# Strided attention on one core: the first fourteen output groups are stored one by one instead of in pairs

## The chip, the cores and the metric

The kernel runs on one core of a Trainium2 chip. Its time is the device time of one execution in microseconds (us). A core has five engines with a stream of instructions each: PE (TensorE, matrix products), DVE (VectorE), ACT (ScalarE), POOL (GpSimd) and SP (SyncE), which here only issues transfers. The transfers are carried out by sixteen DMA engines; SP's instruction ends when a transfer has been handed over, and a semaphore tells later that its data has landed.

## The reference

Every query of a head attends to 16 keys, the rows 0, 64, 128, ... of that head:

```
batch, heads, seq, dim = (8, 12, 1024, 64); stride = 64; float32
for i in range(seq):
    attend_positions = np.arange(0, seq, stride)
    q = Q[:, :, i:i + 1, :]
    k, v = K[:, :, attend_positions, :], V[:, :, attend_positions, :]
    scores = np.einsum('bhqd,bhkd->bhqk', q, k) / sqrt(dim)
    weights = softmax(scores over the 16 keys)
    result[:, :, i, :] = np.einsum('bhqk,bhkd->bhqd', weights, v)
```

So all of Q (96 heads of 256 KB) has to be read and an output of the same size written, and of K and V only 1/64 of the rows.

## The kernel before

**Groups.** The 96 heads are taken four at a time: 24 groups (NG), each with 1 MB of Q and 1 MB of output. K's and V's rows are fetched once, as 384 KB each in rows of 256 bytes.

**A group's way through the core.** SP loads the group's Q into one of ten buffers `qn` (QBUFS = 10). ACT and POOL cast a half each to bfloat16 (L328, L330), DVE transposes (L335, in the loop L449), PE makes the scores (L469), ACT raises them in two halves (L353), PE multiplies with the values in three blocks (L497), and DVE (L453, L459), ACT (L383) and POOL (L385) scale the blocks into one of eight output buffers `out_sb` (OBUFS = 8). POOL's L385 is a group's last work; a store waits for it. Cast, transposition and scores run up to three groups ahead of the outputs.

**What gives buffers back.** A load into `qn` waits until the casts of the group ten earlier are done. The second half of the exponential of group g (L353) waits until the store of group g - 8 has landed; everything that writes the output buffer comes after it. The map `stored` holds which transfer that is.

**The order on SP.** Every transfer goes through SP, which issues strictly in the order of the program. First come K's rows, load 0, V's rows and loads 1 to 9. Then, for each group g in turn, load g + 10 (while g + 10 < 24), and after every second group one store of two groups, 2 MB (two neighbouring output buffers are one tile, so one access pattern covers both). Groups 22 and 23 are stored alone; the last of them stands outside the planned part, at L512. A transfer that waits holds up every later one on SP, loads too.

**Semaphores.** Each load buffer and each pair of output buffers has a semaphore (`lane`) of its own; K's and V's loads borrow two of the stores'. The waits are worked out from the reads and writes that each operation declares (`Program.plan`).

Of the kernel before, what the change touches and what calls it, by code (L numbers as in the profile page):

```python
# [18 lines left out]
def _ap_with(ap: bass.AP, new_ap, extra_offset: int = 0) -> bass.AP:  # L19
    return dataclasses.replace(  # L20
        ap, ap=[list(p) for p in new_ap], offset=ap.offset + extra_offset
    )


def _copy(nc, out: bass.AP, in_: bass.AP):

    sides = [
        mybir.BassSymbolicTensorAccessPattern(
            ap=side.ap, dtype=side.dtype, bass_ap=side,
            is_dma=True, for_custom_bir_dma=True,  # L30
        )
        for side in (in_, out)
    ]
    return nc.sync.add_instruction(
        mybir.InstDMACopy(
            name=nc.get_next_instruction_name(), engine=mybir.EngineType.SP,
            ins=sides[:1], outs=sides[1:], queue="qSPDynamicHW",
            mode="Copy",
        )
    )  # L40


class Program:
# [13 lines left out]
    def op(self, engine, fn, reads=(), writes=(), after=(), lane=None, gate=None, gates=(), looped=False, last=False):  # L57
        i = len(self.ops)
        deps, own = set(after), set()
        for k in reads:  # L60
            deps.add(self.writer.get(k))
            own.add(self.writer.get(k))
        for k in writes:
            deps.update(self.readers.get(k, ()))
            deps.add(self.writer.get(k))
            own.add(self.writer.get(k))
        deps.discard(None)
        for k in reads:
            self.readers.setdefault(k, []).append(i)
        for k in writes:  # L70
            self.writer[k], self.readers[k] = i, []
        self.ops.append(dict(
            engine=engine, fn=fn, lane=lane or engine, deps=deps, own=own,
            gate=gate, gates=gates, last=last, looped=looped or engine == "PE",
        ))
        return i
# [90 lines left out]
def kernel(  # L167
# [16 lines left out]
    NG = B * H // HG  # L184
# [6 lines left out]
    QBUFS = 10  # L191
    OBUFS = 8
# [5 lines left out]
    k_raw = sb.tile([P, NC, D], FP32, name="k_raw")  # L198
    v_raw = sb.tile([P, NC, D], FP32, name="v_raw")
# [22 lines left out]
    op = prog.op  # L222
# [3 lines left out]
    def load(g):  # L226
        n = P if g < 2 else 32
        op("SP", lambda: _copy(
            nc, qn[g % QBUFS],
            _ap_with(Q, [[HG * SD // n, n], [1, HG * SD // n]], g * HG * SD),  # L230
        ), writes=[f"qn{g % QBUFS}{h}" for h in range(2)], lane=f"q{g % QBUFS}")
# [3 lines left out]
    def load_rows(name, tile_, src, lane):  # L235
        op("SP", lambda: nc.sync.dma_start(tile_, _ap_with(src, kv_src)),  # L236
           writes=[name], lane=lane)

    load_rows("k_raw", k_raw, K, f"out{OBUFS // 2 - 2}")
    load(0)  # L240
    load_rows("v_raw", v_raw, V, f"out{OBUFS // 2 - 1}")
    for g in range(1, QBUFS):
        load(g)

# [2 lines left out]
        out=identity, in_=identity, compare_op=ALU.not_equal, fill=1.0, base=0,  # L247
# [3 lines left out]
    for c in range(2):  # L251
        for a in range(2):
            op("POOL", lambda c=c, a=a: nc.gpsimd.tensor_copy(
                out=perm_v[:, c, a],
# [8 lines left out]
        out=s_sel, in_=identity.rearrange("p (h s k) -> p s h k", h=2, s=4),  # L263
        op=ALU.max, axis=mybir.AxisListType.XY,
    ), reads=["identity"], writes=["s_sel"])
    op("POOL", lambda: nc.gpsimd.tensor_copy(  # L266
        out=v_all[:, :, 4 * D :], in_=s_sel.unsqueeze(1).to_broadcast([P, 4, 4])
    ), reads=["s_sel"], writes=["ones"])
    op("POOL", lambda: nc.gpsimd.tensor_copy(
        out=mask, in_=s_sel.unsqueeze(2).to_broadcast([P, 4, D])  # L270
# [45 lines left out]
    def values(g):  # L316
        v = v_bufs[g % 4]
        op("POOL", lambda: nc.gpsimd.tensor_tensor(  # L318
            out=v[:, 0 : 4 * D].rearrange("p (s d) -> p s d", s=4), in0=mask,
            in1=v_rep[:, g // 2, g % 2].unsqueeze(1).to_broadcast([P, 4, D]),  # L320
            op=ALU.mult,
        ), reads=["mask", "v_rep0", "v_rep1"], writes=[f"v{g % 4}"], gate="masked")
# [3 lines left out]
    def cast(g):  # L326
        q, b = qn[g % QBUFS], qb[g % 2]
        op("ACT", lambda: nc.scalar.copy(b[:, half:], q[:, half:]),  # L328
           reads=[f"qn{g % QBUFS}1"], writes=[f"qb{g % 2}1"])
        op("POOL", lambda: nc.gpsimd.tensor_copy(out=b[:, 0:half], in_=q[:, 0:half]),  # L330
           reads=[f"qn{g % QBUFS}0"] + [f"qb{g % 2}1"] * (g >= 2) + ["turn"] * (g < 2),
           writes=[f"qb{g % 2}0"] + ["turn"] * (g < 2), gate="cast")
# [4 lines left out]
    def transpose(g):  # L337
        k_in = {0: "00", 1: "01"}.get(g)
        op("DVE", lambda: turn_over(g),
           reads=[f"qb{g % 2}0", f"qb{g % 2}1"] + [f"k_t{k_in}{s}" for s in range(4) if k_in],  # L340
           writes=[f"qt{g % 2}"], gate="turned", gates=[("cast", g + 1)], looped=g >= 2)

    def scores(g):
        s = g % 2
        op("PE", None,
           reads=[f"qt{g % 2}"] + [f"k_t{int(min(g, NG - 1) >= 8)}{g % 2}{i}" for i in range(4)],
           writes=[f"sc{s}0", f"sc{s}1"], gates=[("turned", g + 1)])
        if g == NG:
            return
        sc, w = sc_ps[s], w_bufs[g % 2]  # L350
        for a in range(2):
            wa = w[64 * a : 64 * a + 64]
            op("ACT", lambda a=a, wa=wa: nc.scalar.activation(  # L353
                out=_ap_with(wa, [wa.ap[0], [P, 8], [1, 2], [2, 32]], extra_offset=64 * a),
                in_=sc[64 * a : 64 * a + 64].rearrange("p (t x q) -> p t x q", t=8, x=2),
                func=AF.Exp, bias=0.0, scale=scale,
            ), reads=[f"sc{s}{a}"], writes=[f"w{g % 2}{a}"], gate="raised" if a else None,
               after=[stored[g - OBUFS]] if a and g >= OBUFS else [])
# [8 lines left out]
    def outputs(g, c):  # L367
        t = (3 * g + c) % 2
        o_key, to_key = f"o{(3 * g + c) % 2}", f"out{g % OBUFS}{c}"
        op("PE", None, reads=[f"w{g % 2}0", f"w{g % 2}1", f"v{g % 4}", "ones"], writes=[o_key],  # L370
           gates=[
               [("raised", g + 1), ("masked", g + 2), ("scaled", 2 * g + 2)],
               [("copied", g + 1)], [("scaled", 2 * g + 3)],
           ][c], gate="out")
        r, o, to, by = parts(g, c)
        r_key = f"rec{g % 2}{c}"
        sums = op("DVE", None, reads=[o_key], writes=[r_key], gates=[("out", 3 * g + c + 3)],
                  gate="own" if c < 2 else None, looped=True)
        if c < 2:
            op("DVE", None, reads=[o_key, r_key], writes=[to_key], gate="scaled",  # L380
               gates=[("own", 2 * g + c + 1)], looped=True)
        else:
            op("ACT", lambda: nc.scalar.copy(to, o), reads=[o_key], writes=[to_key, f"copy{g}"],  # L383
               after=[sums])
            op("POOL", lambda: nc.gpsimd.tensor_tensor(out=to, in0=to, in1=by, op=ALU.mult),  # L385
               reads=[to_key, r_key], writes=[to_key], last=g == NG - 1)

    def send(g, n):
        o = out_sb[g % OBUFS]
        return _copy(  # L390
            nc,
            _ap_with(out, [[16 * D, P], [2 * SD, 2 * n], [1, 16 * D]], g * HG * SD),
            _ap_with(o, [o.ap[0], [1, 1], [1, 32 * n * D]]),
        )

    def store(g, n):
        both = range(g, g + n)
        sent = op("SP", lambda: send(g, n), lane=f"out{g % OBUFS // 2}",
                  reads=[f"out{i % OBUFS}{c}" for i in both for c in range(3)])
        stored.update((i, sent) for i in both)  # L400

# [22 lines left out]
    for g in range(NG):  # L424
        transpose(g + 2)
        if g + 3 < NG:
            cast(g + 3)
        elif g + 1 < NG:
            op("POOL", lambda: nc.gpsimd.nop(), reads=[f"out{(g - 1) % OBUFS}2"], gate="cast")
        if g + 2 < NG:  # L430
            values(g + 2)
        scores(g + 1)
        for c in range(3):
            outputs(g, c)
        if g + 1 < NG:
            op("ACT", lambda: nc.scalar.nop(), reads=[f"copy{g}"], gate="copied")
        if g + QBUFS < NG:
            load(g + QBUFS)
        if g % 2 and g < NG - 2:
            store(g - 1, 2)  # L440
        elif g == NG - 2:
            store(g, 1)

    def dve_stream(sems, gates):
        dve = nc.vector
# [101 lines left out]
```

## Time and profile before

| | |
|---|---|
| three runs | 127.96, 128.0 and 128.7 us; median 128.0 |
| the profiled execution | 127.91 us, of which its first to its last instruction (the span) take 126.1 |
| bytes moved | 51.15 MB: 25.95 read from HBM, 25.17 written |
| granted TensorE clock, mean | 0.883 |
| transfers | 24 loads of 1 MB, 11 stores of 2 MB, 2 stores of 1 MB, K's and V's rows |

The page of the profile gives the busy time of each engine and, in forty slices of the span, the share in which the sixteen DMA engines were busy. The median time from a transfer's issue to its landing was 15.8 us for the loads, 16.6 for the stores of 2 MB and 7.5 for the two of 1 MB. That time holds the wait behind earlier transfers as well as the transfer itself, so it is no measure of a transfer's own length; that is read from the distance between one landing and the next.

### The profile page before, as it was taken

To read this page: it belongs to the slowest core of one execution; us is meant where nothing else is said; L and a number is where in the kernel's file an instruction comes from. 1 tells how busy PE (TensorE), PEld (TensorE's weight loads), DVE (VectorE), ACT (ScalarE), POOL (GpSimd) and SP (SyncE) were. 2 spreads that over 40 slices of the span, in tenths; PEclk is the share of its full clock that TensorE was granted. 3 is DMA by queue.
4 is the path that set the end of the run, shared out by engine and by line. 5 is a ranking of instruction groups with operands and counts; after the bars stand their busy time and mean duration, and the time that the engine had idled before them with its cause. 6 is when DMAs were issued, how large, how long until landed. Compare 5 with 4: busy or idle time off the path is not lost.

```text
span 126.1 us, 1274 instructions
## 1 busy us (share of the span) xinstructions
PE 67.0 (53%) x296; PEld 29.4 (23%) x296; DVE 90.8 (72%) x161; ACT 80.9 (64%) x103; POOL 78.1 (62%) x89
## 2 busy tenths in 40 slices
PE   0005463877946656777655666366277659662000
PEld 0001121433413322333322333132032224330000
DVE  2996356786697999696997999989467746996000
ACT  4260944469667999957899799797199097562000
POOL 4073338278569799949699699979269359344300
PEclk9999999999999999756999999999756855999555
DMA  1999999899999999989989989999999999999992
GB/s 38 346 356 514 416 416 468 385 478 416 416 400 442 436 400 462 436 374 468 416 374 442 452 364 431 473 385 426 447 410 421 426 426 426 431 421 426 413 421 125
DMA packets 6324, 51.15 MB, mean 406 GB/s; under 512 B 3696, under 2 KB 3696, under 8 KB 3696
## 3 DMA queue, kind: packets, MB, share of 16 engines
q1 hardware_dynamic: 6320, 51.12, 97.0%
q14 instruction: 4, 0.03, 0.1%
HBM read 25.95 MB, written 25.17 MB: 405 GB/s over the span
## 4 chain that ended last, share of the span: by engine, by line
DMA 26%; DVE 24%; PE 19%; POOL 10%; ACT 8%; issue 4%; SPq 2%; DVEq 0%; ACTq 0%; POOLq 0%
DMA out_dram<-out_sb 19%; DVE out_sb L459 14%; PE sc L469 10%; PE o L497 9%; DMA qn<-in_Q_dram 7%; DVE qt L335 6%; POOL out_sb L385 5%; ACT out_sb L383 4%; DVE rec L453 4%; POOL qb L330 3%; ACT w_all L353 3%; ACT qb L328 2%; SPq L236 1%; DVE v_rep L312 1%; POOL v_all L318 1%
## 5 line engine op out<-in xcount | busy, mean ns | idle before, releaser
L497 PE MATMUL o<-v_all,w_all 128*128 128x260 bf16 x192 | 38.6, 322 | 30.3 <-DVE out_sb L459 25.1
L385 POOL TENSOR_TENSOR out_sb<-out_sb,rec 128x768 f32<-128x768 f32 x24 | 35.3, 1472 | 28.0 <-ACT out_sb L383 28.0
L469 PE MATMUL sc<-qt,k_t 128*128 128x512 bf16 x100 | 34.0, 472 | 16.5 <-DVE qt L335 12.3
L353 ACT ACTIVATE w_all<-sc 64x512 bf16<-64x512 f32 x48 | 35.2, 733 | 11.1 <-DMA out_dram<-out_sb 7.1
L459 DVE TENSOR_TENSOR out_sb<-o,rec 128x768 f32<-128x768 f32 (+1 forms) x48 | 39.6, 824 | 1.6
L335 DVE STREAM_TRANSPOSE qt<-qb 128x1024 int32<-128x1024 int32 x26 | 31.7, 1220 | 3.8 <-POOL qb L330 3.5
L497 PEld LDWEIGHTS o<-v_all,w_all 128*128 128x128 bf16 x192 | 17.9, 110 | 54.8 <-DVE out_sb L459 33.5
L383 ACT COPY out_sb<-o 128x768 f32<-128x768 f32 x24 | 19.2, 799 | 15.3 <-DVE rec L453 15.0
L328 ACT CAST qb<-qn 128x1024 bf16<-128x1024 f32 x24 | 25.0, 1045 | 4.5 <-DVE v_rep L312 1.7
L330 POOL CAST qb<-qn 128x1024 bf16<-128x1024 f32 x24 | 24.8, 1038 | 2.1 <-DMA qn<-in_Q_dram 2.1
L453 DVE RECIPROCAL rec<-o 128x12 f32<-128x12 f32 (+1 forms) x72 | 15.2, 211 | 13.8 <-PE o L497 13.2
L318 POOL TENSOR_TENSOR v_all<-mask,v_rep 128x256 bf16<-128x256 bf16 x24 | 16.1, 671 | 4.2 <-DVE v_rep L312 4.1
L469 PEld LDWEIGHTS sc<-qt,k_t 128*128 (+1 forms) x100 | 11.1, 112 | 28.1 <-issue 12.3
L257 DVE MEMSET k_t<- 128x3600 uint32 x1 | 3.1, 3058 | 2.3 <-issue 2.3
L312 DVE CAST v_rep<-o 128x768 bf16<-128x768 f32 x2 | 1.9, 938 | 2.9 <-PE o L302 2.9
L291 DVE COPY k_t<-k_r 32x256 bf16<-32x256 bf16 x8 | 3.1, 394 | 0.1
L277 ACT CAST k_bf<-k_raw 128x256 bf16<-128x256 f32 (+1 forms) x2 | 0.9, 508 | 2.8 <-DMA k_raw<-in_K_dram 2.8
L266 POOL COPY v_all<-s_sel 128x16 bf16<-128x16 bf16 x1 | 0.2, 197 | 3.7 <-DVE s_sel L262 3.7
L302 PE MATMUL o<-v_bf,perm_v 128*128 128x384 bf16 x4 | 1.5, 521 | 1.3 <-POOL v_bf L416 1.3
L277 ACT ACT_TABLE_LOAD x1 | 1.3, 1283 | 1.3 <-SPq L143 1.3
L291 ACT COPY k_t<-k_r 32x128 bf16<-32x128 bf16 x4 | 1.2, 295 | 0.5 <-DVE k_r L279 0.5
L291 POOL COPY k_t<-k_r 32x128 bf16<-32x128 bf16 x4 | 1.2, 288 | 0.3
(13 smaller groups left out, 5.1 us busy)
## 6 DMA issues: line engine op xcount, KB each, us to landing
qn<-in_Q_dram SPq DMA_DIRECT2D x24, 1024.0 KB, 15.8
out_dram<-out_sb SPq DMA_DIRECT2D x11, 2048.0 KB, 16.6
out_dram<-out_sb SPq DMA_DIRECT2D x2, 1024.0 KB, 7.5
k_raw<-in_K_dram SPq DMA_DIRECT2D x1, 384.0 KB, 4.5
v_raw<-in_V_dram SPq DMA_DIRECT2D x1, 384.0 KB, 7.0
```

The costliest lines, as they stand in the source:

```text
L291: op(e, lambda: fn(k_t[dst : dst + 32, 2 * part.start + c : 2 * part.stop : 2, :, col : col + NK], k_r[src : src + 32, part].rearrange("p ...
L318: op("POOL", lambda: nc.gpsimd.tensor_tensor(out=v[:, 0 : 4 * D].rearrange("p (s d) -> p s d", s=4), in0=mask, in1=v_rep[:, g // 2, g % 2] ...
L328: op("ACT", lambda: nc.scalar.copy(b[:, half:], q[:, half:]), reads=[f"qn{g % QBUFS}1"], writes=[f"qb{g % 2}1"])
L330: op("POOL", lambda: nc.gpsimd.tensor_copy(out=b[:, 0:half], in_=q[:, 0:half]), reads=[f"qn{g % QBUFS}0"] + [f"qb{g % 2}1"] * (g >= 2) + [ ...
L335: return nc.vector.transpose(qt[g % 2].bitcast(I32), qb[g % 2].bitcast(I32))
L353: op("ACT", lambda a=a, wa=wa: nc.scalar.activation(out=_ap_with(wa, [wa.ap[0], [P, 8], [1, 2], [2, 32]], extra_offset=64 * a), in_=sc[64 ...
L383: op("ACT", lambda: nc.scalar.copy(to, o), reads=[o_key], writes=[to_key, f"copy{g}"], after=[sums])
L385: op("POOL", lambda: nc.gpsimd.tensor_tensor(out=to, in0=to, in1=by, op=ALU.mult), reads=[to_key, r_key], writes=[to_key], last=g == NG - 1)
L453: sums = dve.reciprocal(r, o_ps[(3 * j + c) % 2][:, 0 : blocks[c][1], 4 * D : 4 * D + 4])
L459: dve.tensor_tensor(out=to, in0=o, in1=by, op=ALU.mult).then_inc(gates["scaled"], 1)
L469: r = pe.matmul(sc_ps[g % 2], lhsT=k_t[:, k, f, NK * (1 - e) : NK * (1 - e) + P], rhs=_ap_with(qt[g % 2], [qt[g % 2].ap[0], [D, 8], [16 * ...
L497: r = pe.matmul(o_ps[(3 * j + c) % 2][:, i, 0 : 4 * D + 4], lhsT=w_bufs[j % 2][:, i0 + i], rhs=v_bufs[j % 4], start=True, stop=True,)
```

## The change

Groups 0 to 13, the ones behind which a load is still to be issued, are stored singly, right behind that load. SP's order in the middle becomes load 10, store 0, load 11, store 1, ... load 23, store 13, and then as before: pairs 14-15, 16-17, 18-19, 20-21, and 22 and 23 alone. In the order before it was load 10, load 11, store 0-1, load 12, load 13, store 2-3, and so on. There are eight semaphores for the stores, one for each output buffer, instead of four, and K's and V's loads borrow the last two of them. Each of the groups 8 to 21 now waits for the store of one group. The instructions of PE, DVE, ACT and POOL are the same and stand in the same order; only which semaphore some of ACT's wait for differs. SP issues seven transfers more.

```
-    load_rows("k_raw", k_raw, K, f"out{OBUFS // 2 - 2}")
+    load_rows("k_raw", k_raw, K, f"out{OBUFS - 2}")
     load(0)
-    load_rows("v_raw", v_raw, V, f"out{OBUFS // 2 - 1}")
+    load_rows("v_raw", v_raw, V, f"out{OBUFS - 1}")
...
     def store(g, n):
         both = range(g, g + n)
-        sent = op("SP", lambda: send(g, n), lane=f"out{g % OBUFS // 2}",
+        sent = op("SP", lambda: send(g, n), lane=f"out{g % OBUFS}",
                   reads=[f"out{i % OBUFS}{c}" for i in both for c in range(3)])
         stored.update((i, sent) for i in both)
...
         if g + QBUFS < NG:
             load(g + QBUFS)
-        if g % 2 and g < NG - 2:
+        if g < NG - QBUFS or g == NG - 2:
+            store(g, 1)
+        elif g % 2 and g < NG - 2:
             store(g - 1, 2)
-        elif g == NG - 2:
-            store(g, 1)
```

## The prediction

> **What bounds the kernel now.** I read the page first, for the engine nearest to full.
>
> ```profile
> span 126.1 us, 1274 instructions
> PE 67.0 (53%) x296; PEld 29.4 (23%) x296; DVE 90.8 (72%) x161; ACT 80.9 (64%) x103; POOL 78.1 (62%) x89
> DMA  1999999899999999989989989999999999999992
> q1 hardware_dynamic: 6320, 51.12, 97.0%
> ```
>
> No engine is over 72%, but the sixteen DMA engines are busy for 97.0% of the span, idle only in the first and the last slice. SP has one queue, so the question is whether it ever ran dry. The next view is SP's timeline (start, duration, what is issued), and beside it the time to landing of single transfers, each from a look at the one in whose window the issue falls. The rows of the second fence belong to the issues at 11.00 (load 10), 25.92 (load 11), 30.43, 39.26, 46.73, 53.47, 103.96, 111.57, 114.76 and 118.49 us, in this order.
>
> ```profile
> 11.00 0.52 SPq L34 DMA_DIRECT2D qn<-in_Q_dram  x1
> 25.92 0.47 SPq L34 DMA_DIRECT2D qn<-in_Q_dram  x1
> 30.43 0.63 SPq L34 DMA_DIRECT2D out_dram<-out_sb  x1
> 39.26 0.59 SPq L34 DMA_DIRECT2D out_dram<-out_sb  x1
> 46.73 0.59 SPq L34 DMA_DIRECT2D out_dram<-out_sb  x1
> 53.47 0.59 SPq L34 DMA_DIRECT2D out_dram<-out_sb  x1
> 103.96 0.54 SPq L34 DMA_DIRECT2D out_dram<-out_sb  x1
> 111.57 0.54 SPq L34 DMA_DIRECT2D out_dram<-out_sb  x1
> 114.76 0.54 SPq L34 DMA_DIRECT2D out_dram<-out_sb  x1
> 118.49 0.54 SPq L34 DMA_DIRECT2D out_dram<-out_sb  x1
> ```
>
> ```profile
> qn<-in_Q_dram SPq DMA_DIRECT2D x1, 1024.0 KB, 22.6
> qn<-in_Q_dram SPq DMA_DIRECT2D x1, 1024.0 KB, 10.1
> out_dram<-out_sb SPq DMA_DIRECT2D x1, 2048.0 KB, 10.9
> out_dram<-out_sb SPq DMA_DIRECT2D x1, 2048.0 KB, 12.1
> out_dram<-out_sb SPq DMA_DIRECT2D x1, 2048.0 KB, 14.4
> out_dram<-out_sb SPq DMA_DIRECT2D x1, 2048.0 KB, 17.6
> out_dram<-out_sb SPq DMA_DIRECT2D x1, 2048.0 KB, 11.6
> out_dram<-out_sb SPq DMA_DIRECT2D x1, 2048.0 KB, 8.9
> out_dram<-out_sb SPq DMA_DIRECT2D x1, 1024.0 KB, 8.1
> out_dram<-out_sb SPq DMA_DIRECT2D x1, 1024.0 KB, 6.9
> ```
>
> Issue plus landing time gives when each landed: load 10 at 33.6, load 11 at 36.0, store 0-1 at 41.3, then 51.4, 61.1 and 71.1; at the end store 18-19 at 115.6, 20-21 at 120.5, 22 at 122.9 and 23 at 125.4. The first store was issued at 30.43, when the queue still held work until 36.0, 5.6 us; the last at 118.49, when store 22 had yet to land at 122.9, 4.4 us. These are the thinnest places, so the queue never ran dry, and the time is the sum of what each transfer takes of the DMA engines. The chain of waits (start, length, what) gives the two more landings that the prices need, load 1 at 3.22 + 8.47 = 11.7 and store 12-13 at 76.75 + 24.06 = 100.8:
>
> ```profile
> 3.22 8.47 DMA qn<-in_Q_dram
> 76.75 24.06 DMA out_dram<-out_sb
> ```
>
> **Prices.** Nine loads from load 1 to load 10: (33.6 - 11.7) / 9 = 2.43 us for 1 MB with loads alone. Stores of 2 MB alone: (115.6 - 100.8) / 3 = 4.93. Stores of 1 MB alone: (125.4 - 120.5) / 2 = 2.45. In the mixed stage a round of two loads and a 2 MB store, landing to landing, takes (100.8 - 41.3) / 6 = 9.92, against 2 x 2.43 + 4.93 = 9.79 by the pure prices: 0.13 too much. Single rounds run from 9.7 (51.4 to 61.1) to 10.1 (41.3 to 51.4). The windows (length, busy time of each engine, granted clock, DMA share, GB/s) say the same for loads alone, the mixed stage and stores alone:
>
> ```profile
> 10.90:33.10 22.20, 14.85 (x47) 6.08 (x46) 14.38 (x25) 12.95 (x16) 11.86 (x13) 1.00 1.01 435
> 41.00:99.90 58.90, 36.00 (x180) 16.43 (x179) 50.04 (x91) 47.50 (x59) 46.24 (x45) 0.88 1.00 423
> 99.90:119.50 19.60, 10.70 (x47) 4.37 (x45) 12.12 (x24) 10.07 (x13) 9.63 (x8) 0.76 1.00 425
> ```
>
> 435, 423 and 425 GB/s, all at a DMA share of 1.00 or 1.01: mixing costs little, and there is little to win back.
>
> **The change, part by part.**
>
> *Seven transfers more, each half as long.* Two 1 MB stores cost 2 x 2.45 = 4.90, one of 2 MB 4.93: no difference that these rows resolve, so 0. Landing times are read to 0.1 us, so a single store is known to some 0.05; times 14 that leaves -0.7 to +0.7 at the very worst. SP's issuing, 0.54 to 0.63 us each, is 7 x 0.6 = 4.2 us more, hidden: SP is waiting for a group most of the time, and each issue runs while the queue holds at least 4.4 us.
>
> *More changes of direction.* Loads and stores alternated in six rounds after the first store, and will alternate in thirteen, so seven more. If the whole excess of a round belongs to the turn-round, that is 7 x 0.13 = +0.9. If it belongs to the time spent beside busy engines (DVE, ACT and POOL are far busier in the mixed window than in the other two, 50.04 of 58.90 us for DVE), it does not grow: 0. A round below the pure price (9.7) gives 7 x -0.1 = -0.7, and the worst (10.1) 7 x 0.3 = +2.1. I take the middle of the two readings, +0.45.
>
> *Store 0 earlier, loads 11, 13, ... later.* Load 11 was let go by group 0's end at 25.92; store 0 waits for the same thing and now goes first, load 11 right behind. Nothing is issued later than the queue needs it: load 10 lands at 33.6, store 0 has been there since 25.9; store 1 comes to the head 4.9 us later, at 38.5, and group 1 was done at 30.43; store 3 at 48.3 (done 39.26), store 5 at 58.1 (46.73), store 7 at 67.9 (53.47). The thinnest lead at the start grows from 5.6 to about 7.7 us. A store that waits now has a load behind it on SP that was ahead of it before: load 13 comes after store 2 and lands near 48.5. Its cast is not due before the tenth group; the last load, 23, shows the same at its worst. It was issued at about 70.6 and landed at 95.9 (25.3 later, the longest of all loads); it goes behind store 12, so some 2.5 us later, 98.4. ACT's timeline shows the last cast, which needs it:
>
> ```profile
> DMA to landing us min/median/max: 6.4/15.5/25.3
> 102.50 1.04 ACT L328 CAST qb<-qn 128x1024 bf16<-128x1024 f32 x1
> ```
>
> 98.4 is still 4.1 us ahead of 102.50. If the cast came due earlier than the load, only compute that has a lead over the queue would wait.
>
> *Output buffers come free one group earlier.* ACT's waits for landed stores, and the longest of them:
>
> ```profile
> ACT w_all L353 <- DMA out_dram<-out_sb: 7.1, 3, 3.2
> 100.83 0.73 ACT L353 ACTIVATE w_all<-sc 64x512 bf16<-64x512 f32 x1 [3.24 <-DMA out_dram<-out_sb]
> ```
>
> Group 20 waited here until 100.8 for the pair 12-13; it will wait for store 12 alone, whose place in the queue ends at about 33.6 + 12 x 4.9 + 2.5 + 1 (excess so far) = 96. That takes up to 4.9 us out of the compute chain, which is worth nothing at the end, since the stores are queued 4.4 us deep behind it. Groups 22 and 23 still wait for the pair 14-15 near 105.7, so the last store is ready no later than now.
>
> *Semaphores.* POOL waits for eight stores' semaphores instead of four, while the last transfers run. 0.
>
> Sum against the profiled execution: 127.91 + 0 + 0.45 = 128.36 us; the median of the runs, 128.0, stands 0.1 above that execution, so 128.4.
>
> **The rivals.**
>
> *Turning round is dear* (slower, chance 0.21). Each extra change from stores to loads and back costs what the worst round showed, 0.3 us: 7 x 0.3 = 2.1, 130.1 us. It passes 1%, 1.28 us, from 0.18 a round on. For it: the two kinds of traffic alone run at 435 and 425, mixed at 423, below both. Against: the mean round shows 0.13 and one round none.
>
> *A fixed cost per transfer comes out* (slower, 0.03). The first transfer of all, K's 384 KB, landed 4.5 us after its issue at 0.96; V's, of the same size but queued, 7.0 us after 2.23, at 9.2, only 1.3 us behind load 0 (1.46 + 6.4 = 7.9):
>
> ```profile
> k_raw<-in_K_dram SPq DMA_DIRECT2D x1, 384.0 KB, 4.5
> v_raw<-in_V_dram SPq DMA_DIRECT2D x1, 384.0 KB, 7.0
> ```
>
> So a transfer into an empty queue pays about 4.5 - 1.3 = 3.2 us more. Seven of these would be 22 us, 150 us. It decides only if the queue is empty when a single store is issued, and the leads above are 4.4 us and more. The Trainium skill, DMA: Bandwidth & Descriptors, section Anatomy of one DMA, puts a fixed 2.0 us on a transfer (measured on GpSimd's path), which would by estimate make 7 x 2.0 = 14 us, 142 us, if nothing hid it; the 1 MB stores landing 2.45 us apart at the end show that a filled queue hides it.
>
> *Compute sets the end* (faster, 0.03). If the chain through ACT's wait ended the kernel, store 12 landing up to 4.9 us sooner would give 123 us, or about 125.6 if only half of it arrives. Against: the last store waits 4.4 us behind others after compute is done.
>
> *Finer mixing lets reads and writes overlap* (faster, 0.04). 27 transfers of 1.05 MB at 423 GB/s take 67.0 us, at the loads' 435 65.2: 1.8 less, 126.2 us. Against: the DMA share is 1.00 in the mixed stage already.
>
> **How the numbers follow.** The forecast has the remaining 0.69: 128.4, with 127.6 to 129.2 for it alone (its two readings 0 and +0.9, and some 0.3 around them). A difference of 1%, about 1.3 us, is what a measurement of this kernel can tell from no change. Faster by over 1%: 0.03 + 0.03 (most of the last rival) = 0.06. Slower: 0.21 + 0.03 = 0.24, less 0.02 for the turn-round falling short of 0.18, and 0.01 from the forecast's tail: 0.23. Within 1%: 0.71. The range for 8 in 10 reaches down to 127.2 and up to 129.8, through most of the dear turn-round.
>
> **What will show it.** Right: the DMA share stays at 9 in every inner slice, queue 1 near 97%; a load and a store together land 4.9 to 5.0 us apart from 34 to 100 us; ACT's waits for stores shrink; the last store still lands after one that was queued before it. Wrong: a landing-to-landing distance of 5.1 or more for a load and a store (dear turn-round), slices of 8 or less in the middle (the queue ran dry), or a last store that lands about 3 us after its issue (compute sets the end).

## The result, and the profile after

The changed kernel takes 127.63 us (median of 22 runs, 127.23 to 128.12) against 128.02 for the one before (22 runs, 127.55 to 128.7): a ratio of 0.9966 with a 95% interval of 0.9952 to 0.998. That is 0.4 us faster; the forecast was 128.4, 0.45 us slower than the profiled execution before. The profiled execution after took 127.61 us, of which the span is 125.8.

The page of the kernel after, the same lines as in the prediction:

```profile
span 125.8 us, 1283 instructions
PE 65.3 (52%) x296; PEld 28.9 (23%) x296; DVE 90.8 (72%) x161; ACT 80.8 (64%) x103; POOL 78.1 (62%) x89
DMA  2999979799799999899897998999998999999991
q1 hardware_dynamic: 7328, 51.12, 97.0%
```

The engines are as busy as before, and so is the queue: 97.0% in both. The digits in the DMA row scatter more (a packet counts in the slice in which it starts, and a slice of 3.1 us holds two or three pieces of a load), so the windows decide. Loads alone, the mixed stage, stores alone (length, busy time of each engine, granted clock, DMA share, GB/s):

```profile
10.60:33.00 22.40, 13.84 (x53) 5.53 (x53) 15.87 (x28) 14.39 (x18) 13.13 (x14) 1.00 1.01 433
36.10:99.30 63.20, 41.21 (x203) 19.26 (x202) 54.48 (x101) 52.09 (x66) 50.29 (x50) 0.87 1.01 428
99.30:118.90 19.60, 8.23 (x35) 3.00 (x32) 9.95 (x18) 6.94 (x10) 7.73 (x7) 0.70 1.00 423
```

The mixed stage moves 428 GB/s where it moved 423. In the very same window, 36.1 to 99.3 us, the kernel before moves 424, and the repeats r1 and r2 below move 425 and 428. The other two stages are within 2 GB/s of what they were. The mixed stage is where the time came from.

SP's timeline of the kernel after (start, duration, what), for load 10, stores 0 and 13, the pair 20-21, and stores 22 and 23, and below it the time to landing of each in this order:

```profile
10.65 0.52 SPq L34 DMA_DIRECT2D qn<-in_Q_dram  x1
25.63 0.63 SPq L34 DMA_DIRECT2D out_dram<-out_sb  x1
74.15 0.59 SPq L34 DMA_DIRECT2D out_dram<-out_sb  x1
108.35 0.54 SPq L34 DMA_DIRECT2D out_dram<-out_sb  x1
111.66 0.54 SPq L34 DMA_DIRECT2D out_dram<-out_sb  x1
116.14 0.54 SPq L34 DMA_DIRECT2D out_dram<-out_sb  x1
```

```profile
qn<-in_Q_dram SPq DMA_DIRECT2D x1, 1024.0 KB, 22.6
out_dram<-out_sb SPq DMA_DIRECT2D x1, 1024.0 KB, 10.5
out_dram<-out_sb SPq DMA_DIRECT2D x1, 1024.0 KB, 26.1
out_dram<-out_sb SPq DMA_DIRECT2D x1, 2048.0 KB, 11.8
out_dram<-out_sb SPq DMA_DIRECT2D x1, 1024.0 KB, 10.9
out_dram<-out_sb SPq DMA_DIRECT2D x1, 1024.0 KB, 8.9
```

Store 0 landed at 25.63 + 10.5 = 36.1 and store 13 at 100.2: thirteen rounds of a load and a store in 64.1 us, 4.93 each, or 9.86 for two, where a round before took 9.92. At the end stores 22 and 23 follow the pair 20-21 (120.2) at 122.6 and 125.0, 2.45 us apiece.

**A landing is that of the slowest DMA engine.** A transfer's semaphore counts sixteen increments, one from each DMA engine, and the sixteen engines drift apart. For finer distances I take the mean of the sixteen increments from the trace. From load 10 to the last store that has loads ahead of it, the same 13 loads and 14 MB of stores in both orders, that mean advances by 66.72 us before and 66.31 after: 0.41 us less.

**Pieces.** The trace has every packet with its length. From load 2 on, a load's packets are pieces of 32 KB, two for each DMA engine, and mostly take 1213 to 1219 ns. Those over 1300 ns are called long here. Before, 32 of the 384 after 36 us took over 1300 ns, up to 2147; after, 1 of 400 did (1304). What the pieces took beyond 1216 ns comes to 0.71 us for each DMA engine before and to 0.08 after. Packets follow each other on a DMA engine within a few ns (the largest gap between 11 and 124 us was 0.05 us before and 0.07 after), so a long piece is lost time.

### The profile page after: what moved, and what is told of

Read it like the earlier page. It is cut to its first block, busy times and chain, and to the rows that moved or that the text cites. A ratio compares the mean times of both kernels' runs of the same rounds, so it can differ in the third digit from the quotient of the medians.

```text
span 125.8 us, 1283 instructions
## 1 busy us (share of the span) xinstructions
PE 65.3 (52%) x296; PEld 28.9 (23%) x296; DVE 90.8 (72%) x161; ACT 80.8 (64%) x103; POOL 78.1 (62%) x89
## 4 chain that ended last, share of the span: by engine, by line
DMA 26%; DVE 20%; ACT 14%; PE 14%; POOL 12%; issue 4%; SPq 2%; DVEq 0%; ACTq 0%; POOLq 0%
DMA out_dram<-out_sb 19%; DVE out_sb L459 11%; PE sc L469 7%; DMA qn<-in_Q_dram 6%; PE o L497 6%; POOL out_sb L385 6%; ACT out_sb L383 6%; ACT w_all L353 5%; DVE qt L335 5%; POOL qb L330 4%; ACT qb L328 3%; DVE rec L453 3%; DVE v_rep L312 1%; SPq L236 1%; POOL v_all L318 1%
## 5 line engine op out<-in xcount | busy, mean ns | idle before, releaser
L497 PE MATMUL o<-v_all,w_all 128*128 128x260 bf16 x192 | 37.5, 315 | 29.9 <-DVE out_sb L459 25.0
L469 PE MATMUL sc<-qt,k_t 128*128 128x512 bf16 x100 | 33.3, 464 | 16.5 <-DVE qt L335 12.3
L453 DVE RECIPROCAL rec<-o 128x12 f32<-128x12 f32 (+1 forms) x72 | 15.3, 212 | 11.0 <-PE o L497 10.5
```

The costliest lines, as they stand in the source:

```text
L453: sums = dve.reciprocal(r, o_ps[(3 * j + c) % 2][:, 0 : blocks[c][1], 4 * D : 4 * D + 4])
L469: r = pe.matmul(sc_ps[g % 2], lhsT=k_t[:, k, f, NK * (1 - e) : NK * (1 - e) + P], rhs=_ap_with(qt[g % 2], [qt[g % 2].ap[0], [D, 8], [16 * ...
L497: r = pe.matmul(o_ps[(3 * j + c) % 2][:, i, 0 : 4 * D + 4], lhsT=w_bufs[j % 2][:, i0 + i], rhs=v_bufs[j % 4], start=True, stop=True,)
```

## The experiments

Fourteen runs: both kernels once more (r1, r2) and twelve variants. The table has, for each, the order in the mixed stage (L a load, S a 1 MB store, P a 2 MB store), the advance of the mean increment from load 10 to store 13 or pair 12-13, the count of load pieces over 1300 ns after 36 us, and the ratio to the kernel before with its interval.

| kernel | order | advance, us | long pieces | ratio |
|---|---|---|---|---|
| before, first profile | L L P | 66.72 | 32 | 1 |
| r1, before again | L L P | 66.62 | 28 | 0.9995 (0.9978 to 1.0012) |
| after, first profile | L S | 66.31 | 1 | 0.9966 (0.9952 to 0.998) |
| r2, after again | L S | 66.25 | 1 | 0.9971 (0.9953 to 0.9988) |
| e1, P in 8 KB pieces | L L P | 67.04 | 42 | 1.0023 (1.0002 to 1.0044) |
| e2, blocks of two | L L S S | 67.11 | 35 | 1.0079 (1.0056 to 1.0103) |
| e3, waits for pairs | L S | 66.28 | 3 | 0.9977 (0.9952 to 1.0003) |
| e4, blocks of three | L L L S S S | 66.98 | 42 | 1.0074 (1.0046 to 1.0102) |
| e5, before, loads in 8 KB | L L P | 66.64 | none of 32 KB | 1.0024 (0.9999 to 1.005) |
| e6, after, loads in 8 KB | L S | 66.36 | none of 32 KB | 1.0000 (0.9977 to 1.0023) |
| e7, transfers alone | L L P | 66.64 | 33 | 1.0039 (1.0018 to 1.006) |
| e8, transfers alone | L S | 66.29 | 3 | 1.0014 (0.9983 to 1.0046) |
| e9, halves | half L, half S | not comparable | 66 | 1.0382 (1.0331 to 1.0433) |
| e10, all singles | L S | 66.24 | 0 | 0.9981 (0.9956 to 1.0006) |
| e11, transfers alone | S L L | other stage | 27 | 1.0074 (1.005 to 1.0098) |
| e12, transfers alone | S S L | other stage | 3 | 1.0011 (0.9973 to 1.0049) |

**Both kernels again.** The first pair of profiles differed already before the first changed transfer: load 10 landed at 33.60 us before and at 33.25 after.

> The kernel before once more, unchanged, for the scatter of time and profile. In the first profiles the slowest of the sixteen DMA engines was 0.35 us later before (33.60 us) than after the change (33.25) already when load 10 landed, ahead of the first changed transfer, and 0.30 later at the last landing (125.34 and 125.04). Theory S, the start is a matter of chance: load 10 lands anywhere from 33.2 to 33.7 in this repeat, and the end moves with it. Theory P, the start belongs to the program: 33.6 again. By either, a ratio to before of 1.000 +- 0.001, and loads of the mixed stage with pieces (32 KB each) that take 1300 to 2150 ns instead of 1213, some fifty of them, as in the first profile.

> The changed kernel once more. Theory S: load 10 lands anywhere from 33.2 to 33.7. Theory P: 33.25 again. By either, a ratio to before of 0.9966 +- 0.0015, and hardly any 32 KB piece of a load over 1300 ns once the first store is through.

Load 10 landed at 33.71 and 33.25, as theory P said; but with e1, which starts as the kernel before does, it landed at 33.30, and with e3, which starts as the kernel after, at 33.81. So the start goes with neither order, and the advance is counted from load 10 on. The long pieces and the ratios repeat: 28 and 1, 0.9995 and 0.9971. (The "some fifty" long pieces of the expectation were 32 in the first profile.)

**Is it the smaller pieces, or the order?** Two kernels separate them. e1 is the kernel before with another shape of the store's source:

```
-            _ap_with(o, [o.ap[0], [1, 1], [1, 32 * n * D]]),
+            _ap_with(o, [o.ap[0], [32 * D, n], [1, 32 * D]]),
```

> The kernel before with its 2 MB stores written as pieces of 8 KB instead of 16 KB out of SBUF; order, number and size of the transfers stay. Theory A, the gain is in the finer alternation of loads and stores: ratio 1.000 to 1.001, and the stretched load pieces (over 1300 ns) stay. Theory B, the gain is in the smaller pieces that the singles are made of: ratio 0.996 to 0.997, the stretched load pieces gone. Theory C, the gain is in buffers that come free one by one: 1.000.

e2 is the changed kernel with the singles issued in twos:

```
-        if g < NG - QBUFS or g == NG - 2:
-            store(g, 1)
+        if g % 2 and g < NG - QBUFS:
+            store(g - 1, 1)
+            store(g, 1)
+        elif g < NG - QBUFS:
+            pass
+        elif g == NG - 2:
+            store(g, 1)
```

> Groups 0 to 13 stored singly, but in the order of before: two loads, then two 1 MB stores. Theory A (alternation): ratio 0.999 to 1.001, stretched load pieces stay. Theory B (pieces of 8 KB): 0.996 to 0.997, stretched pieces gone. Theory C (buffers one by one): part of the gain, 0.998, for half of the groups get their buffer a transfer sooner.

Theory B falls with both: 42 and 35 long pieces, ratios 1.0023 and 1.0079. e2 has the transfers of the changed kernel, all of them, and is 1.0 us slower than the kernel before; only by being issued one by one do they become faster. That is theory A's side, though A did not expect e2 to lose so much.

**Do buffers that come free earlier help?** e3 lets ACT wait for both stores of a pair, in the order after the change:

```
-            ), ..., after=[stored[g - OBUFS]] if a and g >= OBUFS else [])
+            ), ..., after=[stored[g - OBUFS], stored[(g - OBUFS) | 1]] if a and g >= OBUFS else [])
```

> The changed kernel with one more wait: the exponential of group g waits for the stores of both groups of the pair that g - 8 belongs to, as before the change; order and size of the transfers are those after it. Theory C (the gain is in buffers that come free one by one): ratio to before 1.000. Theory A (the gain is in the order, one load then one store): 0.9966 +- 0.0015, as if nothing had been added, with ACT waiting longer for landed stores.

The advance is 66.28 and the long pieces are 3, as with the changed kernel, so theory C is not what shortens the mixed stage, though ACT waits 8.1 us for landed stores in e3 and 4.1 in the changed kernel. The ratio alone, 0.9977 with 1 inside its interval, could not have told.

**How does the loss go with the order?** e4 issues three loads, then three stores, and so has the fewest changes of direction.

```
+            if g % 3 == 2:
+                store(g - 2, 1)
+                store(g - 1, 1)
+                store(g, 1)
+            elif g == NG - QBUFS - 1:
+                store(g - 1, 1)
+                store(g, 1)
```

> Singles in blocks of three: three loads, then three 1 MB stores, and so on. Pairs of singles were 1.0 us slower than before (ratio 1.0079), one by one is 0.4 faster. Theory D, the first load after a store is unharmed and every load behind another load loses, so that the loss goes with the number of such loads: none one by one, 6 in blocks of two, 8 in blocks of three: ratio about 1.010, stretched load pieces in second and third loads. Theory E, one loss for each block of loads that is longer than one (6 blocks of two, 4 of three): about 1.004. Theory F, a loss for each change of direction, the one I predicted from: fewest changes here, so 0.994 or less.

1.0074: theory F, the one I predicted from, is out by more than 1%. D and E expected 1.010 and 1.004; the ratio lies between, so it does not decide them. Sorted by load, the long pieces speak against D as it was put: about 35 of the 42 lie in the third loads, the last before the stores, and only a handful in the second loads, which stand directly behind a load too.

**Is it the long pieces of the loads?** e5 and e6 are the kernels before and after with loads in pieces of 8 KB:

```
-        n = P if g < 2 else 32
+        n = P
```

> The kernel before with its loads in pieces of 8 KB (one for each partition) instead of 32 KB; order and stores of before. Theory G, the stretching belongs to the long pieces of the loads: the mixed stage loses nothing any more, ratio 0.995 to 0.998. Theory H, it belongs to the order, whatever the pieces: 0.999 to 1.002. The price of smaller pieces as such is small by the stores (8 KB pieces at 310 ns, 16 KB at 616), below 0.3 us in all.

> The changed kernel with its loads in pieces of 8 KB. Theory G: no stretched pieces were left to remove, so the same as the changed kernel, 0.9966 +- 0.0015; the lag of the slowest DMA engine behind the mean, 1.2 us at the end, stays. Theory I, the lag comes from the loads' long pieces as well: the lag shrinks to some 0.5 us and the ratio goes to 0.991 to 0.994. Theory H: 0.9966 to 0.999.

No: e5 keeps its 66.64, and some 8 KB pieces now take up to 959 ns instead of 310. Theory H. The pieces as such cost something: in the stage of loads alone a load takes 2.45 us in e5 and in e6, by the mean increments of loads 1 to 10, against 2.43 in the kernels before and after. e6 keeps the short mixed stage (66.36) and yet loses the gain of the change (1.0000); 0.2 us of that is this price up to load 10, and the rest no run shows.

**Is an engine in SBUF in the way?** e7 and e8 have the transfers alone, in the two orders; all computation is left out, and the output is a constant. Their core, for e8:

```
        for g in range(NG):
            if g + QBUFS < NG:
                load(g + QBUFS)
            if g < NG - QBUFS or g >= NG - 2:
                store(g, 1)
            elif g % 2:
                store(g - 1, 2)
```

> Transfers alone, in the order of before (two loads, then a 2 MB store): all loads and stores, no work on PE, ACT and POOL, and the output buffers filled once with a constant by DVE, so the output is not attention. A load waits only for the landing of the loads ten and five earlier. Theory J, the stretched load pieces come from the transfers among themselves: some thirty pieces over 1300 ns in the mixed stage, as in the kernel before, and the mixed stage 0.3 to 0.6 us longer than in the next kernel. Theory K, they come from the engines working in SBUF beside the transfers: no stretched pieces, and the two kernels within 0.1 us.

> The same, transfers alone, in the order after the change (one load, one 1 MB store, pairs when no loads are left). The same work is left out. Theory J: hardly any piece over 1300 ns, and 0.3 to 0.6 us faster than the kernel of transfers alone in pairs. Theory K: the two within 0.1 us.

Windows of the mixed stage, 36.0 to 99.3 us, first of the transfers in pairs (e7), then of the singles (e8); the columns are length, busy time of DVE and of POOL, granted clock, DMA share and GB/s:

```profile
36.00:99.30 63.30, 0.00 (x0) 0.00 (x0) 1.00 1.00 425
```

```profile
36.00:99.30 63.30, 0.00 (x0) 0.00 (x0) 1.00 1.01 427
```

No engine does anything in this stage, and the difference is there all the same: 33 long pieces and 3, an advance of 66.64 and 66.29, 0.35 us apart where the full kernels are 0.41 and 0.37 apart. Theory J: the transfers do it among themselves. The times of e8 lie between 127.40 and 129.45 us, so its ratio is of little use. Both profiles caught the slowest execution of their kernel (129.38 and 129.45 us), and in that of e8 a single DMA engine ended 1.8 us behind the others (124.05 for the fifteenth, 125.85 for the last). So it is the count of long pieces that carries this reading, and e11 repeats it below without any computation.

**Is finer still better?** e9 cuts each load and each store of groups 0 to 13 into halves of 64 partitions, in turn:

```
+            for h in range(2):
+                load_half(g + QBUFS, h)
+                store_half(g, h)
```

> The changed kernel with still finer alternation: each load and each store of groups 0 to 13 goes in two halves of 64 partitions, half a load, half a store, in turn. Theory D (only a load behind a load loses): nothing left to gain, ratio 0.9966 +- 0.002. Theory F (each change of direction costs, the one I predicted from): twice the changes of the kernel after it, so slower than that by what thirteen more rounds cost, 1.0 or more. Theory L (the finer the better): 0.993 to 0.995.

3.8% slower (132.0 to 133.8 us in four executions, 134.75 and 137.28 in two), with 66 long pieces. Only theory F had forecast a slower kernel, and thirteen more rounds at its 0.13 us make 1.7 us, not the 4.9 seen against the kernel before. Theory D fails here: no load stands directly behind a load in this order, and there are more long pieces than in any other run. The run does not tell the grain apart from the halves: it also changes which partitions a transfer touches. The Trainium skill, DMA: Bandwidth & Descriptors, section Rules for kernel authors, advises against two transfers to disjoint halves of the partitions, because both use all sixteen DMA engines anyway; that they are dear in this order, the page does not say and this run shows.

**All singles.** e10 stores groups 14 to 21 singly as well:

```
-        if g < NG - QBUFS or g == NG - 2:
+        if g < NG - 1:
             store(g, 1)
-        elif g % 2 and g < NG - 2:
-            store(g - 1, 2)
```

> The changed kernel with groups 14 to 21 stored singly too, where no loads are left. By the landings a 1 MB store costs as much as half of a 2 MB one, and the order stays, so every theory gives 0.9966 +- 0.0015; if a price per transfer came out after all, four more at the end would show it (0.998 or more).

The ratio, 0.9981, lies at the mark that was set for a price, and its interval holds the changed kernel's 0.9966 too, so it decides nothing. The advance is 66.24, as after the change. From store 13 to the last store the mean increment advances by 24.65 us here, by 24.56 and 24.57 in the two profiles after: some 0.1 us for four more transfers. On the slowest DMA engine it is 25.09 against 24.83 in both.

**Loads in a row, or stores in a row?** With transfers alone the order is free, so the two can be separated. e11 has six times one store and two loads, e12 six times two stores and one load; computation is left out as in e7.

```
        for r in range(6):                      # e11
            store(r, 1)
            load(QBUFS + 2 + 2 * r)
            load(QBUFS + 3 + 2 * r)
...
        for r in range(6):                      # e12
            store(2 * r, 1)
            store(2 * r + 1, 1)
            load(18 + r)
```

> Transfers alone again (no work on PE, ACT and POOL, constant output), all stores of groups 0 to 13 of 1 MB: twelve loads, then six times one store and two loads, then the stores that are left. Here loads stand behind loads and no store behind a store while loads are mixed in. Theory D (a load behind a load, after a store, loses): stretched load pieces over 1300 ns, 15 to 40. Theory M (it is the stores in a row that do it, by what they leave behind them): none or a few, as in the order one by one.

> The same transfers with eighteen loads first, then six times two stores and one load, then the stores that are left: stores behind stores, and no load behind a load. The same work is left out. Theory D: hardly any piece over 1300 ns in the mixed stage. Theory M: 15 to 40 of them.

27 long pieces with loads in a row, 3 with stores in a row; of these 3, two lie in the last load ahead of the first store, and one in the mixed stage. The windows of the mixed stages (e11, then e12; same columns as above):

```profile
38.30:82.50 44.20, 0.00 (x0) 0.00 (x0) 1.00 1.00 420
```

```profile
52.50:96.70 44.20, 0.00 (x0) 0.00 (x0) 1.00 1.01 427
```

The same transfers take 128.93 us in the first order and 127.71 in the second (medians; three of e12's ten executions took 128.9 to 129.3). In e11 the last increments of the last store spread from 123.62 to 125.84 us, in e12 from 123.49 to 124.05. Theory M falls: a store directly behind a store makes no pieces long. Theory D holds between these two orders: it takes loads in a row in a stage where stores are mixed in.

**Which load has the long pieces.** The rule of theory D can be made narrower from the traces. In the kernel before, all but one or two of the 32 long pieces lie in the second load of a round; in r1 at least 20 of 28 do, in e7 26 of 33, in e11 about 25 of 27; in e4 it is the third load. In the stage of loads alone, 0 to 7 pieces are long in these profiles and in r2 (7), and all of them lie in the last load ahead of the first store. So a load mostly loses when a load stands directly ahead of it and a store directly behind it. It is not the whole rule: in e1 about half of the long pieces lie in first loads, and e9 has long pieces with no load behind a load.

## Why the prediction was wrong

**What bounds the kernel: right.** The queue never ran dry: the largest gap on a DMA engine was 0.07 us. The last store was issued at 116.14, when store 22 had yet to land at 122.6.

**Seven more transfers cost nothing: right.** The last two stores take 2.45 us each after the change as before it. In the mixed stage, counted from the start of a packet to the start of the next, the fourteen single stores take 0.1 us more than seven pairs, and in the repeat nothing; e10's four more cost some 0.1 us. All of this is inside the 0.7 us that the prediction allowed.

**More changes of direction, +0.45 us: this step failed, in its sign.** It took the excess of a mixed round, 0.13 us, and split it between turning round and time spent beside busy engines. It belonged to neither. The long load pieces come to 0.71 us for each DMA engine over the six rounds before, 0.12 a round; in the repeat to 0.50, or 0.08. That is nearly the whole excess in the first profile, and more than half of it in the repeat. With whole loads and stores they come with loads in a row (e11 against e12), they do not need a busy engine (e7), and they do not grow with the changes of direction, which doubled while the pieces went from 32 to 1. The order after the change has no load behind a load once stores are mixed in, so the excess was taken away instead of multiplied. The term should have been about -0.13 x 6 = -0.8 for the whole excess at the most; the advance shows -0.41, -0.37 in the repeat. That the time stayed within 1%, as forecast, is owed to the small size of the term, not to its mechanism.

**Why the gain isn't more.** The stores took little of it: a piece of 8 KB is recorded with 311 ns where half of a 16 KB one has 308, but packets overlap by some 3 ns, and from start to start the usual distances are 307 ns and 613, twice 306.5. Counted so, the 13 loads won 0.60 us and the 14 MB of stores lost 0.12; in the repeat the loads won 0.44 and the stores nothing. More than the long pieces had cost, 0.71 and 0.50 us, was not to be won from them. And the end is set by one DMA engine. The sixteen increments of the last store came between 123.57 and 125.34 us before. After, fifteen came by 124.21 and the last at 125.04 (in the repeat by 124.40, and at 125.11). Nearly fifty of that engine's pieces of 8 KB in the mixed stage took 313 to 352 ns, so that its mean is 318 against 311 on another; why, no run shows.

**Store 0 earlier, buffers free sooner, worth nothing: right.** The waits of ACT after the change:

```profile
ACT w_all L353 <- DMA out_dram<-out_sb: 4.1, 3, 2.6
```

7.1 us became 4.1, the last store was issued 2.35 us sooner (118.49 to 116.14), and it only stood longer in the queue: 8.9 us to its landing instead of 6.9. e3 puts the waits back and keeps the shorter mixed stage. Load 23 landed at 71.42 + 26.3 = 97.7, near the 98.4 that was worked out.

**The rivals.** Dear turning round is refuted by the change itself, with thirteen turns and 4.93 us for a load and a store where 5.1 was to be its sign; e4, which turned least often, lost 0.7%. A fixed cost for each transfer did not show, and compute did not set the end. Finer mixing had the right sign and the wrong mechanism: no piece became shorter than in the stages of one kind, there are only fewer long ones, and mixing finer still (e9) was slower, if for a reason that stays open.

**What stays open.** What makes a piece long at all: the order says when, not why, and e9 and half of e1 do not fit it. Why e2, in the order before with smaller stores, loses 1.0 us against it: its load pieces lose 1.00 us for each DMA engine (0.71 before, 0.50 in r1), and the sixteen increments of its last store are 2.85 us apart (1.77 before). And what the one late DMA engine does. No version tried beats the changed kernel.

## What to carry to other kernels

Where a queue is full from end to end, the time is the sum of the pieces on the slowest DMA engine, and the order in the queue can change the pieces: look for packets of one size that take longer than their kind before pricing a change of order by an average round. An excess seen in a mixed stage must be tied to something that can be counted (changes of direction, loads behind loads, engines at work) before it is multiplied by anything. When loads and stores of 1 MB share one full queue, let one load and one store follow each other in turn; here that was worth 0.3%.

## What the runs showed of the hardware that was not expected

- A load directly behind another load, with stores mixed in, had 32 KB pieces of up to 2.1 us instead of 1.22 (32 of 384 before), with no engine at work as well (33 of 384 in e7); most of them lay in the last load ahead of a store. One load and one store in turn had 1 of 400, two stores and one load 3 of 368.
- The sixteen DMA engines run on their own: at the end of the kernel before they were 1.77 us apart, in e2 2.85, and in e12 0.56.
- Loads and stores in halves of 64 partitions, in turn, cost 3.8% (e9), with 66 long pieces.
